# New written orders for the long filter and the mixer's second half, and another place for the throwaway product of the first FFN's modulation sums

## The chip, the cores and the metric

The kernel runs on one core of a Trainium2 chip. The metric is the device time of one execution in microseconds (us). The engines are TensorE (PE, matrix products; PEld is its weight load), VectorE (DVE), ScalarE (ACT) and GpSimd (POOL); SyncE (SP) issues DMAs. The engines run their own instruction lists and wait for each other by semaphores.

## The reference

Two layers of a diffusion transformer over 512 image positions (`x`) and 256 context positions (`ctx`), width 1024. Layer 0 mixes by a Fourier transform and a long convolution, layer 1 by latent attention. Each layer is modulated by vectors that are computed from a condition (`c`, `c_ctx`): six of 1024 each.

```python
def _adaln(cond, w_mod, b_mod):
    mod = jax.nn.silu(cond) @ w_mod + b_mod
    return jnp.split(mod[:, None, :], 6, axis=-1)

def _long_conv(u, spectrum, bias):
    L = u.shape[1]
    y = jnp.fft.irfft(jnp.fft.rfft(u, n=2 * L, axis=1) * spectrum[None], n=2 * L, axis=1)[:, :L]
    return y + u * bias

def _fourier_hyena_mixer(h, w_in, w_out, conv_w, conv_b, w1, b1, w2, b2, w3, b3, w4, freq, hy_bias):
    proj = h @ w_in
    u_f = proj[..., :D_FOURIER].reshape(B, L, 4, 128)
    y_f = jnp.fft.fft2(u_f, axes=(1, 3), norm='ortho').real.reshape(B, L, D_FOURIER)
    u_h = _dwconv3(proj[..., D_FOURIER:], conv_w, conv_b)
    x0, x1, v = jnp.split(u_h, 3, axis=-1)
    spectrum = _hyena_filter_spectrum(L, w1, b1, w2, b2, w3, b3, w4, freq)
    y_h = x0 * _long_conv(v * x1, spectrum, hy_bias)
    return jnp.concatenate([y_f, y_h], axis=-1) @ w_out

def reference(...):
    for i in range(2):
        sh1, sc1, g1, sh2, sc2, g2 = _adaln(c, w_mod[i], b_mod[i])
        hx = _modulate(_rms_norm(x, norm1[i]), sh1, sc1)
        ...
        x = x + g1 * yx
        x = x + g2 * _conv_ffn(_modulate(_rms_norm(x, norm2[i]), sh2, sc2), *ffn)
        ...
    return x
```

The context goes through the same steps with its own modulation (until the last layer's attention).

## The kernel before, in words

**Layout.** Activations lie transposed: 1024 features as eight tiles of 128 partitions, positions along the free axis (512 image columns and 256 of the context, 772 with padding). The tiles `x0` to `x7` of pool `xp` hold the input rows at first. Later in the mixer the first four hold `x0` of the reference, and the last four, called `Uf`, hold the Fourier channels; `Uf[3]` is `x7`.

**Products.** Every large product is made of three: a weight tile is split into a high part `wh` (ACT, L191) and a remainder `wl` (DVE, L196), an activation likewise, and `mm3` issues high by high (L216), high by low (L217) and low by high (L218). A 128 by 1024 weight arrives by an SP DMA as `wr`. Pool `W` keeps three each of `wr`, `wh` and `wl`. Accumulators are `mm` (1024 columns, three buffers) and `ms` (512 columns, two).

**The stages up to the first FFN.** (1) The norm of the input and a small network for the filter, in an order of their own. (2) The *filter*: the filter's taps, their transform, and five of the input projections, which are spread among them. (3) The *remaining in-projections*: seven with a convolution of three taps after each (L432 on ACT, L434 to L436 on DVE), the product and folding of their results, and transposes. (4) The *second half*: projections 11, 6 and 7, the forward transform of the folded product, its multiplication by the spectrum, the inverse transform, and the two transforms of the Fourier channels. (5) The *output projection* `res_proj(0, 2, ...)`: eight rows of `w_out` for the image columns, each closed by a residual addition on DVE (`xr`, L1212) and followed by the next norm's square sums (`nt`, L332), then the context's columns. After that come the first FFN and layer 1.

**What sets the order.** Stages 2 and 4 run in the order of the tables `FILTER_ORDER` and `MIX_ORDER`. Each token is one step, and under `manual_schedule` PE, DVE, ACT and POOL each run their instructions in the order in which the tokens issue them. SP's loads and stages 3 and 5 are placed by the framework. An engine never runs a later instruction of its list past a waiting one.

Tokens of the filter that are spoken of: `MM05` and the like make taps of two tiles; `U0`, `U1` copy Fourier channels out of their accumulators (ACT); `P40` is the first quarter of projection 4; `SPAx2` and `SPBx2` are the two halves of the transform for frequency tile x2, both into one `mm` accumulator; `SDAx2` and `SDBx2` scale these halves into SBUF (DVE, L760); `CB4` and `CC4` are the DVE steps of projection 4's convolution (L790, L792); `G0` to `G5` are modulation blocks.

Tokens of the second half: `P70` to `P73` are quarters of projection 7; `SC0`, `SC1` (context) and `SX0` to `SX3` (image) are tiles of the forward transform, `mm` accumulators all; `DA`, `DB` multiply one by the spectrum (DVE, L985 to L988) and release it; `QA`, `QB` add (POOL); `YA`, `YB` and `LA`, `LB` split the result into high and low (`LA` on DVE, `LB` on POOL); `IC0` to `IC3` and `IX0` to `IX3` are the inverse transform; `FA`, `FB` (image) and `GA`, `GB` (context) are the two transforms of Fourier group 0 to 3, with the splits `PH`/`PL` and `GH`/`GL` between them and the sums `FE`/`FS` and `GE`/`GS` (L1102 to L1109) behind; `TH`, `TL` split the cosine and sine tables `ct`, `st`; `FH`, `FL` split a Fourier group; `ZH`, `ZL` split its result into `yh`, `yl`; `OA` and `OB0` to `OB3` are the output projection's first row. `HP` closes the pools of the projections' inputs, whose space the tables and `y` take.

**Modulation sums.** The modulation of the first FFN and of layer 1 is computed on DVE. `gemv_dve` handles one block of 128 outputs: it multiplies a row block of `wmodT` by the broadcast condition `sb`, sums along the row (L301), for the image's condition and for the context's, and adds the bias (L302). The elementwise product itself isn't needed; it goes to a bf16 tile `junk` of 1024 columns, which has one buffer of its own. 32 blocks belong to layer 0's remaining modulation: sixteen are done up to the start of stage 4, eight more by `hook` after the rows of stage 5, one after each row, and eight in the FFN. `junk` depends on nothing else, so the framework may issue such a sum as soon as its weights can be loaded.

Of the kernel before, what the change touches and what calls it, by code (L numbers as in the profile page):

```python
# [101 lines left out]
Rc0 THc0 THs0 YBx0 YAx0 Rn0 CC7 LBx0 IC2 FL0 TLs0 Rc1 IC3 THn0 LAx0 GA0 DAx1 DBx1 QAx1 SX2 GH0 QBx1 FA0 GL0 TLc0 THc1 YAx1 YBx1
LBx1 LAx1 FH1 TLn0 TLc1 DAx2 DBx2 SX3 PH0 GB0 ICM0 FH2 QAx2 QBx2 PL0 YAx2 ICH0 YBx2 LAx2 FL1 DAx3 GE0 ICE2 LBx2 DBx3 ICL0 FL2 FB0 FA1 FE0 GS0 PH1 QAx3
Ri1 GA1 QBx3 FS0 ICM1 PL1 YBx3 ICH1 FA2 WHi1 ICL1 ICE3 FB1 ICS2 LBx3 WLi1 GH1 YAx3 PH2 GL1 GA2 LAx3 Ro0 FE1 IX1 PL2 GB1 ICS3 ICM2 IXE1 IX0 IXS1 FH3
FS1 ICH2 ICM3 GH2 ICH3 ICL2 IXM1 IXH1 IXE0 ICL3 IX2 GE1 IXS0 FB2 FL3 GS1 IXE2 IXM0 GL2 FA3 FE2 IXH0 IXS2 IX3 IXM2 IXH2 FS2 GA3 PH3 IXL1 IXL0 PL3 IXL2
# [32 lines left out]
class Builder:  # L138
# [152 lines left out]

        return turn

    def gemv_dve(self, i, jt, conds=(0, 1), raw=None):

        nc = self.nc
        raw = raw or self.wraw(self.I["wmodT"][i, jt])
        for j in conds:
# [2 lines left out]
            nc.vector.scalar_tensor_tensor(junk, raw, 1.0, self.sb[:, j, :], op0=ALU.mult, op1=ALU.mult, accum_out=acc)  # L301
            nc.vector.tensor_tensor(self.mod[i][:, jt, j : j + 1], acc, self.col(f"bm_{i}", jt), op=ALU.add)  # L302
# [1899 lines left out]
```

## Time and profile before

| | us |
|---|---|
| runs | 1555.84, 1561.79, 1557.8 |
| median of the runs | 1557.8 |
| the profiled execution, its own time | 1557.68 |
| its span in the profile | 1555.9 |
| filter (stage 2) | 69.1 to 135.6 |
| remaining in-projections (stage 3) | 135.6 to 199.7 |
| second half (stage 4) | 199.7 to 299.5 |
| output projection, image rows (stage 5) | 299.5 to 338 |

The stages are named by PE's first matmul of each. In a row of the timeline stand the start, the duration, the engine, the line, the operation, the tiles written and read, and in brackets how long the engine had been idle before and what ended this. Matmuls are pipelined, so that a row's duration is longer than the distance to the next start. A row of the groups has the count, the busy time, the mean duration in ns, and the idle time before.

### The profile page before, as it was taken

The page shows a single profiled execution, that of the slowest core. Times are in us where ns is not written, and L with a number is a line of the kernel's source. Part 1 is how long each engine was busy: PE and PEld are TensorE (multiplying, and loading weights), DVE is VectorE, ACT ScalarE, POOL GpSimd, SP SyncE. Part 2 cuts the span into 40 slices and gives each one's busy share as a digit, 9 for nine tenths or more (in the row PEclk, how much of TensorE's full clock was granted, in tenths as well). Part 3 has the DMA queues.
Part 4 walks back from the last instruction along what each step waited for, and adds up shares of the span by engine and source line. Part 5 has one row for each costly group of instructions (what it writes and reads, how often), then busy time and mean ns, then how long its engine had stood idle before and what let it go on. Part 6 is the DMA issues. An engine that isn't in the chain of part 4 may idle for free.

```text
span 1555.9 us, 21217 instructions
## 1 busy us (share of the span) xinstructions
PE 1525.5 (98%) x8456; PEld 1271.6 (82%) x8456; DVE 1037.8 (67%) x1755; ACT 604.7 (39%) x875; POOL 95.8 (6%) x110
## 2 busy tenths in 40 slices
PE   7999998999999999999999999999999999999999
PEld 5788888888888888888888897766569888888887
DVE  6699969878988356663365388999977543444343
ACT  4361224424323212322133246989854432233231
POOL 0121135000000000000000000201200000000000
PEclk9999999999999999999999999999999999999999
DMA  9336502542544235441343220000043223322222
GB/s 367 128 108 228 177 26 77 191 134 94 164 163 157 69 108 172 159 142 63 105 156 115 81 78 21 11 14 14 1 136 109 82 97 100 101 95 95 95 83 94
DMA packets 54111, 171.48 MB, mean 110 GB/s; under 512 B 6139, under 2 KB 9533, under 8 KB 52989
## 3 DMA queue, kind: packets, MB, share of 16 engines
q1 hardware_dynamic: 54013, 170.13, 32.9%
q8 instruction: 67, 1.10, 0.3%
q14 instruction: 31, 0.25, 0.1%
HBM read 164.34 MB, written 5.77 MB: 109 GB/s over the span
## 4 chain that ended last, share of the span: by engine, by line
PE 85%; DVE 8%; issue 2%; ACT 2%; DMA 2%; POOL 1%; SPq 0%; ACTq 0%; DVEq 0%; POOLq 0%
PE mm L216 23%; PE mm L217 23%; PE mm L218 23%; PE pv L1733 3%; DVE junk L301 2%; PE s L216 2%; PE pv L1744 1%; PE s L217 1%; PE s L218 1%; DVE wl L196 1%; PE k L216 1%; PE k L217 1%; PE k L218 1%; DMA wr<-wmodT 1%; PE ms L1637 1%
## 5 line engine op out<-in xcount | busy, mean ns | idle before, releaser
L191 ACT ACTIVATE wh<-wr 128x1024 fp32r<-128x1024 f32 (+1 forms) x184 | 189.7, 1034 | 526.8 <-PE mm L217 450.6
L216 PE MATMUL mm<-hh,wh 128*128 128x512 f32 (+1 forms) x856 | 332.5, 388 | 4.2 <-DVE tm L436 1.7
L217 PE MATMUL mm<-hl,wh 128*128 128x512 f32 (+1 forms) x856 | 330.5, 386 | 2.3 <-DVE hl L371 2.3
L218 PE MATMUL mm<-hh,wl 128*128 128x512 f32 (+1 forms) x856 | 330.0, 386 | 0.0
L196 DVE TENSOR_TENSOR wl<-wr,wh 128x1024 fp32r<-128x1024 f32 (+1 forms) x184 | 222.0, 1209 | 127.1 <-ACT wh L191 121.4
L301 DVE SCALAR_TENSOR_TENSOR junk<-wr,sb 128x1024 bf16<-128x1024 f32 x128 | 157.9, 1234 | 54.7 <-DMA wr<-wmodT 54.4
L216 PEld LDWEIGHTS mm<-hh,wh 128*128 128x128 f32 x856 | 160.9, 188 | 37.7 <-issue 5.9
L218 PEld LDWEIGHTS mm<-hh,wl 128*128 128x128 f32 x856 | 160.8, 188 | 32.7
L217 PEld LDWEIGHTS mm<-hl,wh 128*128 128x128 f32 x856 | 160.9, 188 | 32.2 <-DVE hl L371 3.3
L1212 DVE SCALAR_TENSOR_TENSOR xr<-mm,mod,xr 128x512 f32<-128x512 f32 (+1 forms) x88 | 56.0, 652 | 165.5 <-PE mm L218 163.9
L216 PE MATMUL mm<-hhc,wh 128*128 128x256 f32 (+1 forms) x488 | 135.9, 279 | 0.0
L217 PE MATMUL mm<-hlc,wh 128*128 128x256 f32 (+1 forms) x488 | 135.9, 279 | 0.0
L218 PE MATMUL mm<-hhc,wl 128*128 128x256 f32 (+1 forms) x488 | 135.6, 278 | 0.0
L217 PE MATMUL mm<-al,wh 128*128 128x512 f32 x328 | 127.7, 389 | 0.0
L218 PE MATMUL mm<-ah,wl 128*128 128x512 f32 x328 | 127.7, 389 | 0.0
L216 PE MATMUL mm<-ah,wh 128*128 128x512 f32 x328 | 127.6, 389 | 0.0
L216 PEld LDWEIGHTS mm<-hhc,wh 128*128 128x128 f32 x488 | 91.7, 188 | 3.9
L217 PEld LDWEIGHTS mm<-hlc,wh 128*128 128x128 f32 x488 | 91.6, 188 | 3.9
L218 PEld LDWEIGHTS mm<-hhc,wl 128*128 128x128 f32 x488 | 91.9, 188 | 0.0
L1263 DVE TENSOR_TENSOR fg<-fg,mm 128x768 f32<-128x768 f32 (+1 forms) x44 | 36.1, 821 | 74.9 <-PE mm L218 69.3
L1261 ACT ACTIVATE fg<-fg 128x768 f32<-128x768 f32 (+1 forms) x44 | 32.6, 740 | 134.6 <-DVE fg L436 100.5
L218 PEld LDWEIGHTS mm<-ah,wl 128*128 128x128 f32 x328 | 61.6, 188 | 12.8
(441 smaller groups left out, 2808.1 us busy)
## 6 DMA issues: line engine op xcount, KB each, us to landing
wr<-w_up SPq DMA_DIRECT2D x88, 512.0 KB, 3.4
wr<-wmodT SPq DMA_DIRECT2D x80, 512.0 KB, 3.4
wr<-w_dn SPq DMA_DIRECT2D x32, 512.0 KB, 3.4
wm<-wmod0a SPq DMA_DIRECT2D x8, 1024.0 KB, 9.3
wr<-w_in SPq DMA_DIRECT2D x16, 512.0 KB, 3.4
wr<-w_out SPq DMA_DIRECT2D x13, 512.0 KB, 3.6
wr<-w_dn SPq DMA_DIRECT2D x17, 384.0 KB, 3.0
wr<-w_o SPq DMA_DIRECT2D x8, 512.0 KB, 3.5
```

Source lines behind the costliest of these rows:

```text
L191: self.nc.scalar.activation(dst, src, AF.Copy)
L196: (eng or self.nc.vector).tensor_tensor(dst, src, hi.bitcast(F32), op=ALU.subtract)
L216: mmul(out, wh, xh, start=start, stop=False)
L217: mmul(out, wh, xl, start=False, stop=False)
L218: mmul(out, wl, xh, start=False, stop=stop)
L301: nc.vector.scalar_tensor_tensor(junk, raw, 1.0, self.sb[:, j, :], op0=ALU.mult, op1=ALU.mult, accum_out=acc)
L1212: nc.vector.scalar_tensor_tensor(x[m][:, a2:b2], ps[:, a2 + o : b2 + o], mod[:, 8 * sec + m, c : c + 1], x[m][:, a2:b2], op0=ALU.mult, op1 ...
L1261: nc.scalar.activation(g[:, :n], g[:, :n], AF.Silu)
L1263: v.tensor_tensor(a[:, :n], g[:, :n], pss[1][:, :n], op=ALU.mult)
L1637: nc.tensor.matmul(c.s.rt[:, o : o + 2], c.ks[:, t0 : t0 + 128], ksel, start=True, stop=True)
L1733: nc.tensor.matmul(c.P[64 * a : 64 * a + 64, :], V[:, j, o : o + 64], c.S[a, j // 3][:, j % 3, :], start=j == 0, stop=j == 5, tile_positio ...
L1744: nc.tensor.matmul(c.zz[o : o + 32, :], self.ones32, c.S[a, h][:, i, :], start=i == 0, stop=i == 2, tile_position=(0, o))
```

## The change

Three edits. Both tables hold the same tokens as before in another order. `gemv_dve` takes an argument `row`, and with `row="x7"` the throwaway product goes to the first half of a tile in `x7`'s space, so that the sum comes after the last reader of `x7` (`ZH3` and `ZL3`). And `hook` calls it 0, 1, 1, 1, 2, 1, 1, 1 times after rows 0 to 7 instead of once after each. The number of instructions on each engine is the same, and so are their shapes. Line numbers after L90 are lower by two.

```diff
 FILTER_ORDER = """
-R3 WH3 U1 D0 U2 Ra WL3 WHa Rb P30 WLa MM05 P31 D1 R5 PMb0 PMb5 MM42 PMa5 U0 PMa0 P32 P33 HI5 LO5 PMb4 D2 PMb2 SB PMa4
...
-SPBx1 SQc0 WLx2 CSx SPAx1 RCx SSx SPAx2 WLx0 Sx G1 WH4 WL4 SPBx2 SPBx0 P40 NYx P41 SDBx1 SDBx3 SK2 SPAx0 P42 SDAx3 RG2
-SDAx1 G2 SDBx2 RG3 SQx3 G0 G3 KBx3 NDx SQx1 SDAx2 SQx2 WH6 KAx1 WL6 SDAx0 KBx2 KAx2 RG4 G4 P43 KAx3 CA4 SQx0 CB4 CC4
-KBx1 SDBx0
+MM05 Rb U0 U1 SK1 R3 WH3 D2 RG5 WL3 P30 Ra U2 R5 D0 P31 MM42 PMa0 PMb5 WHb P32 SB PMb0 PMa5 D3 G5 HI5 LO5 D1 WHa PMb4 P33 PMa4 RR4 PMa2 RR0 Z4 WLb RG1
...
+NDc SDAc1 SDBc1 WHx3 WLx3 P43 RG4 CA4 SQc1 SPAx3 CSx WLx1 CB5 R6 WHx2 CB4 CC4 WHx0 CC5 RCx WLx2 SPBx3 SSx G0 Sx SPAx1 WLx0 G3 SK2 G4 WH6 SPBx1 SDAx1
+SPAx2 SDBx1 NDx SQx1 SDAx2 SDAx3 SQx2 KAx1 KBx1 SPBx2 WL6 SPAx0 SDBx2 KAx2 SDAx0 SQx0 KBx2 SPBx0 SDBx3 SQx3 SDBx0 KAx3 KBx3
 """
 MIX_ORDER = """
-P11 R6 R7 WH6 WL6 P60 CA11 P61 CB11 CC11 P62 FM Ru0 WH7 FD T3 P63 WHu0 UH CA6 WL7 UL WLu0 CB6 SC0 Ru1 CC6 DBc0 SC1 DAc1 QBc0 YBc0 LBc0 WHu1 Ri0 Rn1
...
+P11 R6 R7 WH6 WL6 Ru0 P60 P61 P62 WHu0 CA11 WLu0 WH7 CB11 CC11 FM FD T3 P63 Rc0 UH UL SC1 WL7 DAc1 QAc1 CA6 P70 P71 DBc1 SC0 FH0 P72 P73 HP THc0 QBc1
+TLc0 CB6 YAc1 LAc1 YBc1 LBc1 FL0 DBc0 DAc0 Rc1 Ri0 THc1 WHi0 QBc0 Rs0 THs0 SX0 CA7 QAc0 YBc0 TLc1 CC6 Ru1 WLi0 TLs0 YAc0 DBx0 LAc0 LBc0 QBx0 DAx0 SX1
+Rn1 YBx0 QAx0 IC1 ICE1 CB7 ICS1 DAx1 GA0 Rn0 IC3 IC0 WHu1 ICM1 THn0 GH0 ICE0 GL0 CC7 ICS0 ICM0 WLu1 THn1 ICE3 LBx0 FA0 QAx1 DBx1 YAx1 FH1 PH0 ICH0
...
+GL3 WHo0 WLo0 GE2 IXH3 IXE0 GB3 IXS0 IXM0 GS2 IXH0 FE3 IXL3 ZH0 IXL0 OA FS3 GE3 ZH1 ZL0 ZH2 OB0 GS3 ZH3 ZL1 ZL2 OB1 OB2 ZL3 OB3
 """
-    def gemv_dve(self, i, jt, conds=(0, 1), raw=None):
+    def gemv_dve(self, i, jt, conds=(0, 1), raw=None, row=None):
...
-            junk = self.t(self.sbp, [P, D], BF16, "junk", 1)
+            junk = self.t(self.xin, [P, TW], F32, row)[:, : D // 2].bitcast(BF16) if row else self.t(self.sbp, [P, D], BF16, "junk", 1)
...
-        xp = self.pool("xp", side="right")
+        xp = self.xin = self.pool("xp", side="right")
...
         def hook(stage, j, m):
             if stage == 0:
-                if len(gl) > 8:
-                    self.gemv_dve(*gl.pop(0))
+                for _ in range((0, 1, 1, 1, 2, 1, 1, 1)[j]):
+                    self.gemv_dve(*gl.pop(0), row="x7")
                 if j == 7:
                     self.make_A(0, 1)
             nhook(stage, j, m)
```

The order on the engines at three places.

PE where the filter's frequency tile x2 goes from its first half (`a0h`, `a0l`) to its second (`a1h`, `a1l`). Before:

```order
L216 MATMUL mm_1156<-a0h_938,wh_1051 128x512
L217 MATMUL mm_1156<-a0l_939,wh_1051 128x512
L218 MATMUL mm_1156<-a0h_938,wl_1052 128x512
L216 MATMUL mm_1156<-a1h_993,wh_1051 128x512
L217 MATMUL mm_1156<-a1l_994,wh_1051 128x512
```

Now:

```order
L214 MATMUL mm_1276<-a0h_968,wh_1189 128x512
L215 MATMUL mm_1276<-a0l_969,wh_1189 128x512
L216 MATMUL mm_1276<-a0h_968,wl_1190 128x512
L214 MATMUL mm_1276<-a1h_1006,wh_1189 128x512 [waits DVE_49]
L215 MATMUL mm_1276<-a1l_1007,wh_1189 128x512
```

The second half's first matmul now waits for DVE, whose reading of the first half (`SDAx2`) is written ahead of it. It is the same at x0.

DVE near the start of the second half, in the forward transform's multiplications (`sx`). Before:

```order
L934 SCALAR_TENSOR_TENSOR x_19_118<-mm_2001,pcol_67,x_19_118 128x771 [waits DVE_49]
L985 TENSOR_TENSOR sx_2096<-mm_2086,s_266_1088 128x512 [waits PE_49]
L986 TENSOR_TENSOR sx_2097<-mm_2086,s_270_1097 128x512
L988 TENSOR_TENSOR sx_2097<-mm_2086,s_262_1055 1x512 [waits DVE_49]
L985 TENSOR_TENSOR sx_2108<-mm_2101,s_256_1042 128x512 [waits PE_49]
L986 TENSOR_TENSOR sx_2109<-mm_2101,s_257_1044 128x512
L196 TENSOR_TENSOR wl_2118<-wr_2093,wh_2117 128x1024 [waits DMAHW2_49,Activation_49]
```

Now:

```order
L984 TENSOR_TENSOR sx_2125<-mm_2085,s_276_1143 128x512
L194 TENSOR_TENSOR ctl_2213<-wr_2081,cth_2212 128x520 [waits DMAHW2_49,PE_49,Activation_49]
L930 SCALAR_TENSOR_TENSOR x_19_118<-mm_2003,pcol_67,x_19_118 128x771
L194 TENSOR_TENSOR s_468_2221<-sx_2093,s_467_2220 128x512 [waits Activation_49]
L194 TENSOR_TENSOR wl_2136<-x_21_120,wh_2135 128x772
L983 TENSOR_TENSOR sx_2229<-mm_2128,s_267_1083 128x512 [waits DVE_49,PE_49]
L984 TENSOR_TENSOR sx_2230<-mm_2128,s_261_1026 128x512 [waits Pool_49]
L986 TENSOR_TENSOR sx_2230<-mm_2128,s_275_1140 1x512 [waits DVE_49]
```

The first split of the cosine table (`ctl`, token `TLc0`) and that of a Fourier group (`wl<-x_21`, `FL0`) now stand between the multiplications of the two context tiles; `ctl` waits for DMA, PE and ACT.

DVE from the end of the second half to the first residual addition (`xr_612`). Before:

```order
L301 SCALAR_TENSOR_TENSOR junk_3164,gacc_3165<-wr_3162,sb_87 128x1024 [waits DMAHW7_49]
L302 TENSOR_TENSOR mod_4_73<-gacc_3165,pcol_67 128x1 [waits DVE_49]
L301 SCALAR_TENSOR_TENSOR junk_3168,gacc_3169<-wr_3162,sb_87 128x1024
L1107 TENSOR_TENSOR x_24_123<-e_2949,mm_2924 128x128 [waits Activation_49]
L1108 TENSOR_TENSOR x_24_123<-e_2949,mm_2924 128x127
L1109 COPY x_24_123<-e_2949 128x1
L196 TENSOR_TENSOR yl_601_2942<-x_21_120,yh_600_2941 128x772 [waits Activation_49]
L196 TENSOR_TENSOR yl_603_2944<-x_22_121,yh_602_2943 128x772 [waits Activation_49]
L196 TENSOR_TENSOR yl_605_2946<-x_23_122,yh_604_2945 128x772 [waits Activation_49]
L196 TENSOR_TENSOR yl_607_2948<-x_24_123,yh_606_2947 128x772 [waits Activation_49]
```

Now:

```order
L194 TENSOR_TENSOR yl_599_2934<-x_21_120,yh_598_2933 128x772 [waits PE_49,Activation_49]
L1105 TENSOR_TENSOR x_24_123<-e_2970,mm_2916 128x128 [waits Activation_49]
L1106 TENSOR_TENSOR x_24_123<-e_2970,mm_2916 128x127
L1107 COPY x_24_123<-e_2970 128x1
L194 TENSOR_TENSOR yl_601_2936<-x_22_121,yh_600_2935 128x772 [waits Activation_49]
L194 TENSOR_TENSOR yl_603_2938<-x_23_122,yh_602_2937 128x772 [waits Activation_49]
L194 TENSOR_TENSOR yl_605_2940<-x_24_123,yh_604_2939 128x772 [waits Activation_49]
L299 SCALAR_TENSOR_TENSOR x_658_3110,gacc_3111<-wr_3108,sb_87 128x1024 [waits DMAHW4_49,DVE_49]
L1210 SCALAR_TENSOR_TENSOR xr_612_3018<-mm_2954,mod_4_73,xr_612_3018 128x512 [waits DMAHW0_49,PE_49]
```

The modulation sums write to `x_658` (the space of `x7`) instead of `junk`, and all stand behind the last split of `yl`. Before, six of them (three blocks) stood among the second half's steps.

More of the change, by code (lines that the diff above doesn't have):

```diff
@@ L90 @@
 FILTER_ORDER = """
-R3 WH3 U1 D0 U2 Ra WL3 WHa Rb P30 WLa MM05 P31 D1 R5 PMb0 PMb5 MM42 PMa5 U0 PMa0 P32 P33 HI5 LO5 PMb4 D2 PMb2 SB PMa4
-AB5 MM31 SK1 RR4 RR0 PMa2 WHb Z4 D3 HI4 MX5 U3 LO4 RG1 SPAc0 WLb AB4 SPBc0 RG5 Z0 PMb1 Rx3 MX4 HI2 WH5 Rx1 PMa1 PMb3
-SPAc1 Rx2 SPBc1 PMa3 HI1 HI3 LO2 Rx0 WL5 Qc CSc NYc LO1 RCc AB2 P50 P51 HI0 SSc AB1 G5 WHx3 Sc LO3 MX2 P52 R4 R6 LO0
-WLx3 AB0 SDAc1 SDBc1 WHx1 AB3 WHx2 SQc1 NDc P53 CA5 MX3 SPAx3 MX0 SDBc0 WLx1 MX1 Q23 WHx0 SDAc0 SPBx3 CB5 CC5 Q01 Qx RG0
-SPBx1 SQc0 WLx2 CSx SPAx1 RCx SSx SPAx2 WLx0 Sx G1 WH4 WL4 SPBx2 SPBx0 P40 NYx P41 SDBx1 SDBx3 SK2 SPAx0 P42 SDAx3 RG2
@@ L96 @@
-SDAx1 G2 SDBx2 RG3 SQx3 G0 G3 KBx3 NDx SQx1 SDAx2 SQx2 WH6 KAx1 WL6 SDAx0 KBx2 KAx2 RG4 G4 P43 KAx3 CA4 SQx0 CB4 CC4
-KBx1 SDBx0
+MM05 Rb U0 U1 SK1 R3 WH3 D2 RG5 WL3 P30 Ra U2 R5 D0 P31 MM42 PMa0 PMb5 WHb P32 SB PMb0 PMa5 D3 G5 HI5 LO5 D1 WHa PMb4 P33 PMa4 RR4 PMa2 RR0 Z4 WLb RG1
+AB5 PMb2 R4 Rx1 RG2 HI4 WLa Rx3 MM31 LO4 MX5 U3 PMa3 PMa1 SPAc1 AB4 NYc MX4 HI2 PMb3 WH5 SPBc1 SPBc0 PMb1 Rx0 Z0 G1 Qc CSc HI1 Rx2 WH4 HI3 WL5 RCc
+SPAc0 LO1 LO3 LO2 RG0 P50 HI0 AB3 LO0 WL4 AB1 SSc Sc RG3 SDAc0 G2 AB0 P51 P52 NYx P53 SDBc0 WHx1 AB2 MX2 MX1 MX3 Q23 P40 MX0 P41 P42 SQc0 Q01 Qx CA5
@@ L98 @@
+NDc SDAc1 SDBc1 WHx3 WLx3 P43 RG4 CA4 SQc1 SPAx3 CSx WLx1 CB5 R6 WHx2 CB4 CC4 WHx0 CC5 RCx WLx2 SPBx3 SSx G0 Sx SPAx1 WLx0 G3 SK2 G4 WH6 SPBx1 SDAx1
+SPAx2 SDBx1 NDx SQx1 SDAx2 SDAx3 SQx2 KAx1 KBx1 SPBx2 WL6 SPAx0 SDBx2 KAx2 SDAx0 SQx0 KBx2 SPBx0 SDBx3 SQx3 SDBx0 KAx3 KBx3
 """
 MIX_ORDER = """
-P11 R6 R7 WH6 WL6 P60 CA11 P61 CB11 CC11 P62 FM Ru0 WH7 FD T3 P63 WHu0 UH CA6 WL7 UL WLu0 CB6 SC0 Ru1 CC6 DBc0 SC1 DAc1 QBc0 YBc0 LBc0 WHu1 Ri0 Rn1
-P70 QAc1 YAc1 WLu1 P71 DAc0 P72 QAc0 P73 YAc0 WHi0 SX0 LAc1 DBc1 HP QBc1 Rs0 LAc0 WLi0 SX1 CA7 YBc1 THn1 LBc1 CB7 DBx0 IC0 QBx0 ICE0 DAx0 ICS0 IC1 QAx0 ICE1 TLn1 ICS1 FH0
@@ L102 @@
[L102 to L105, printed above, removed]
@@ L106 @@
-IXE3 IXS3 GB2 WHo0 IXM3 IXH3 FB3 GH3 GE2 FE3 WLo0 GL3 GB3 GE3 ZH0 IXL3 GS2 FS3 GS3 OA ZL0 OB0 ZH1 ZL1 ZH2 ZH3 OB1 ZL2 ZL3 OB2 OB3
+P11 R6 R7 WH6 WL6 Ru0 P60 P61 P62 WHu0 CA11 WLu0 WH7 CB11 CC11 FM FD T3 P63 Rc0 UH UL SC1 WL7 DAc1 QAc1 CA6 P70 P71 DBc1 SC0 FH0 P72 P73 HP THc0 QBc1
+TLc0 CB6 YAc1 LAc1 YBc1 LBc1 FL0 DBc0 DAc0 Rc1 Ri0 THc1 WHi0 QBc0 Rs0 THs0 SX0 CA7 QAc0 YBc0 TLc1 CC6 Ru1 WLi0 TLs0 YAc0 DBx0 LAc0 LBc0 QBx0 DAx0 SX1
+Rn1 YBx0 QAx0 IC1 ICE1 CB7 ICS1 DAx1 GA0 Rn0 IC3 IC0 WHu1 ICM1 THn0 GH0 ICE0 GL0 CC7 ICS0 ICM0 WLu1 THn1 ICE3 LBx0 FA0 QAx1 DBx1 YAx1 FH1 PH0 ICH0
@@ new lines @@
+QBx1 IC2 LAx1 PL0 TLn0 SX2 YAx0 ICL0 ICE2 TLn1 ICS3 ICM3 GB0 GE0 GS0 ICH3 YBx1 LBx1 Ri1 ICH1 FB0 FL1 FA1 FE0 DBx2 QBx2 PH1 FS0 YBx2 DAx2 LAx0 SX3 FH2
+PL1 GA1 GH1 LBx2 FB1 QAx2 WHi1 DAx3 Ro0 ICS2 FE1 QAx3 YAx2 GL1 DBx3 GB1 FL2 GA2 YAx3 FS1 QBx3 FA2 YBx3 PH2 ICL1 WLi1 LAx2 ICM2 ICH2 LAx3 PL2 LBx3 IX1
+IX2 IXE1 GH2 IXS1 GE1 GL2 IXE2 FB2 ICL2 GS1 FH3 FE2 IX3 IXM1 IXH1 ICL3 IXS2 FL3 IXM2 GA3 FA3 IXE3 IXL1 FS2 IXH2 IXS3 GB2 IXM3 IXL2 PH3 IX0 PL3 FB3 GH3
+GL3 WHo0 WLo0 GE2 IXH3 IXE0 GB3 IXS0 IXM0 GS2 IXH0 FE3 IXL3 ZH0 IXL0 OA FS3 GE3 ZH1 ZL0 ZH2 OB0 GS3 ZH3 ZL1 ZL2 OB1 OB2 ZL3 OB3
```

## The prediction, made before the changed kernel ran

> **What bounds the kernel now.** I read the page first: busy shares, then the chain of waits.
>
> ```profile
> span 1555.9 us, 21217 instructions
> PE 1525.5 (98%) x8456; PEld 1271.6 (82%) x8456; DVE 1037.8 (67%) x1755; ACT 604.7 (39%) x875; POOL 95.8 (6%) x110
> PE 85%; DVE 8%; issue 2%; ACT 2%; DMA 2%; POOL 1%; SPq 0%; ACTq 0%; DVEq 0%; POOLq 0%
> ```
>
> PE sets the end, and the change takes no matmul away. So only PE's waits and its clock can move the time. By the order, the rows that move on PE and DVE lie between some 60 and 340 us; the rest of the program reads alike. I cut that stretch into its stages (filter, remaining in-projections, second half, output projection), and a part of the second half into pieces. A row has the window and its length, then the busy time (and instructions) of PE, PEld, DVE, ACT and POOL, the granted clock, the DMA share and GB/s.
>
> ```profile
> 69.10:135.60 66.50, 66.50 (x335) 52.27 (x334) 57.49 (x94) 30.17 (x46) 14.27 (x10) 1.00 0.42 139
> 135.60:199.70 64.10, 60.88 (x355) 53.55 (x354) 57.69 (x103) 15.49 (x17) 9.62 (x7) 1.00 0.58 193
> 199.70:299.50 99.80, 92.93 (x599) 84.08 (x598) 87.46 (x150) 42.59 (x71) 30.87 (x36) 0.97 0.23 75
> 299.00:338.00 39.00, 39.00 (x170) 31.62 (x170) 27.26 (x51) 9.51 (x12) 0.00 (x0) 1.00 0.62 207
> 236.56:239.97 3.41, 2.38 (x22) 2.27 (x21) 3.41 (x9) 2.34 (x6) 2.94 (x2) 1.00 0.00 0
> 239.97:243.38 3.41, 3.41 (x18) 3.41 (x17) 3.41 (x6) 1.36 (x3) 3.41 (x2) 0.50 0.42 123
> 243.38:246.80 3.42, 3.42 (x12) 2.84 (x11) 3.23 (x6) 2.24 (x4) 2.60 (x3) 0.50 0.10 38
> ```
>
> The filter has no PE idle to give: 66.50 of 66.50. The in-projections lack some 3.2 us, the second half some 6.9, and the output projection nothing. In the second half PE also ran 6.83 us at a granted clock of 0.50, behind a piece in which it was busy 2.38 of 3.41 us; full speed would save at most half, 3.4 us. The single waits, with what ended them:
>
> ```profile
> 144.25 0.47 PE L216 MATMUL mm<-hh,wh 128*128 128x512 f32 x1 [0.30 <-DVE x L792]
> 171.84 0.47 PE L216 MATMUL mm<-hh,wh 128*128 128x512 f32 x1 [1.68 <-DVE tm L436]
> 190.69 0.47 PE L216 MATMUL mm<-hh,wh 128*128 128x512 f32 x1 [1.24 <-ACT tm L432]
> 218.27 0.50 PE L218 MATMUL mm<-uTh,wl 128*128 128x512 f32 x1 [0.46 <-DVE wl L196]
> 238.69 0.30 PE L216 MATMUL ms<-wh,s 128*128 128x128 f32 x1 [1.03 <-DVE e L1029]
> 260.58 0.36 PE L216 MATMUL mm<-csh,wh 128*128 128x256 f32 x1 [1.21 <-DVE x L1108]
> 263.79 0.39 PE L216 MATMUL mm<-cth,pqh 128*128 128x258 f32 x1 [0.83 <-DVE pql L196]
> 290.81 0.37 PE L216 MATMUL mm<-cth,pqh 128*128 128x130 f32 x1 [1.49 <-DVE pql L1081]
> 296.39 0.50 PE L217 MATMUL mm<-yl,wh 128*128 128x512 f32 x1 [0.96 <-DVE yl L196]
> ```
>
> All but one are ended by DVE. The largest gain to be had is then 3.22 us of waits in the in-projections and 5.98 + 3.4 = 9.4 in the second half, 12.6 in all.
>
> **The change part by part.** *Filter, end.* In the new table DVE's scaling SDAx2 of one half of a frequency tile is written before PE's SPBx2, and SDAx0 before SPBx0, and the order shows the first matmul of each second half with a wait on DVE. Before, both halves ran through. A round trip is built from these rows:
>
> ```profile
> 101.19 0.40 PE L217 MATMUL mm<-a0l,wh 128*128 128x512 f32 x1
> 101.43 0.39 PE L218 MATMUL mm<-a0h,wl 128*128 128x512 f32 x1
> L760 DVE TENSOR_TENSOR s<-mm,S 128x512 f32<-128x512 f32 x11 | 7.2, 682 | 0.0
> 143.09 1.02 DVE L792 SCALAR_TENSOR_TENSOR x<-mm,pcol,x 128x771 f32<-128x771 f32 x1
> ```
>
> Matmuls start 0.24 us apart but last 0.40, so draining costs 0.16; the convolution that ends at 144.11 releases PE at 144.25, a handover of 0.14, paid twice; the scaling takes 0.68. That is 1.1 each, 2.2 for both, if DVE stands ready. It may not: the stage has it busy 57.49 of 66.50 us, and one modulation sum of 1.22 (row below) in front of either scaling would add that. Bounds +2.2 and +5; I take +2.6, near the free round trip, since the order has a wait on PE at the scaling and no sum between it and the PE work it follows for x2. *Filter, start:* taps before the fourth projection, with two copies first that ACT (30.17 of 66.50 busy) hides: 0, and by the nearest row of a stage that waited for its first operand, 0.46, if they are late.
>
> *In-projections.* The convolution steps CB4, CC4 and the sum G4 go ahead of the filter's last scalings, so DVE enters this stage with less behind it. The waits of 0.30 and 1.68 are for convolutions that DVE finishes late: I take −2.0 (bounds −2.0 and 0). The 1.24 is for ACT, whose order stays.
>
> *Second half, what goes.* Six sums, three blocks of modulation, leave its queue; they go to rows of the output projection. Their first and last start here, with the rows they collide with:
>
> ```profile
> 266.72 1.22 DVE L301 SCALAR_TENSOR_TENSOR junk<-wr,sb 128x1024 bf16<-128x1024 f32 x1
> 293.78 1.22 DVE L301 SCALAR_TENSOR_TENSOR junk<-wr,sb 128x1024 bf16<-128x1024 f32 x1
> L302 DVE TENSOR_TENSOR mod<-gacc,pcol 128x1 f32<-128x1 f32 x6 | 0.9, 158 | 0.1
> L196 DVE TENSOR_TENSOR ctl<-wr,cth 128x520 fp32r<-128x520 f32 x2 | 1.9, 940 | 0.0
> L196 DVE TENSOR_TENSOR s<-sx,s 128x512 fp32r<-128x512 f32 x6 | 4.7, 778 | 0.7 <-ACT s L191 0.7
> L985 DVE TENSOR_TENSOR sx<-mm,s 128x512 f32<-128x512 f32 x12 | 8.1, 678 | 0.0
> L932 DVE SCALAR_TENSOR_TENSOR x<-mm,pcol,x 128x771 f32<-128x771 f32 x2 | 2.0, 1014 | 0.2 <-ACT x L930 0.2
> L196 DVE TENSOR_TENSOR wl<-x,wh 128x772 fp32r<-128x772 f32 x4 | 4.9, 1224 | 0.0
> 246.91 1.57 POOL L196 TENSOR_TENSOR s<-sx,s 128x512 fp32r<-128x512 f32 x1 [0.74 <-ACT s L191]
> 247.25 1.79 DVE L196 TENSOR_TENSOR stl<-wr,sth 128x520 fp32r<-128x520 f32 x1
> 238.47 0.67 DVE L196 TENSOR_TENSOR stl<-wr,sth 128x504 fp32r<-128x504 f32 x1
> ```
>
> That is 6 × 1.22 + 0.9 = 8.2 us of a DVE that has 87.46 of 99.80 filled. It would pay for the waits at 260 to 296 (4.5 us together), which the table also attacks by issuing the splits of the cosine and sine tables (TLc0, TLs0, TLc1) and FL0 earlier. So the most that can come back is the 9.4.
>
> *Second half, what comes.* The earlier splits stand in front of work that PE awaits. TLc0's row waits on PE, for the projection P71 whose inputs' space it writes; DBc0 and DAc0, which free the accumulator of SX0, stand behind it. From P71's end DVE has ctl 0.94, CB6 1.01, LAc1 0.78, FL0 1.22 and five products of 0.68: 7.35 us. PE has SC0, six steps of 0.24, and two quarters of a projection, an estimated 2.1 each (a quarter has six steps of 0.24 and six of half the columns): 5.6. SX0 then waits up to 1.8; I take 1.5, since neighbours on DVE overlap by 0.08 each. By the same count IC1 waits for LAc0 behind TLc1, CC6, WLi0 and TLs0 between 0 and 1.3 (0.6), FA0 for GL0 and SX2 for WLu1 0.4 each, and GB0 for TLn0 0.5 to 2.3 (1.4). What I see no reason to lose are the old 0.46 at the transform's start and the 0.96 at the end: together 5.7, so this stage gives 9.4 − 5.7 = 3.7. Bounds: −9.4 if every wait goes, +0.7 if the early splits meet POOL's multiplications. For that two rows speak: a split took 1.79 us while POOL subtracted, and 0.67 elsewhere (520 and 504 columns); 1.1 more on each of the four is 4.4, and 5.7 + 4.4 − 9.4 = 0.7.
>
> The Trainium skill, "SBUF — State Buffer", section "Who interferes with whom", says that a DVE operation with two SBUF inputs excludes a GpSimd one that reads SBUF, whichever is first. It speaks against this change, which puts four such splits where POOL has work; the 1.79 beside 0.67 agrees with it, and by it this stage ends at its upper bound.
>
> *Output projection.* Eight blocks instead of five, sixteen sums. Its rows:
>
> ```profile
> L301 DVE SCALAR_TENSOR_TENSOR junk<-wr,sb 128x1024 bf16<-128x1024 f32 x10 | 12.2, 1223 | 0.5 <-DMA wr<-wmodT 0.5
> L196 DVE TENSOR_TENSOR wl<-wr,wh 128x1024 fp32r<-128x1024 f32 x6 | 7.4, 1226 | 0.7 <-ACT wh L191 0.6
> L1212 DVE SCALAR_TENSOR_TENSOR xr<-mm,mod,xr 128x512 f32<-128x512 f32 x8 | 6.0, 752 | 9.3 <-PE mm L218 7.9 <-DMA xr<-xT 1.4
> L332 DVE TENSOR_TENSOR nt<-nt,nt 128x512 f32<-128x512 f32 x7 | 4.8, 691 | 2.0 <-ACT nt L325 2.0
> 332.55 0.75 DVE L1212 SCALAR_TENSOR_TENSOR xr<-mm,mod,xr 128x512 f32<-128x512 f32 x1 [1.69 <-PE mm L218]
> 338.11 0.75 DVE L1212 SCALAR_TENSOR_TENSOR xr<-mm,mod,xr 128x512 f32<-128x512 f32 x1 [3.35 <-PE mm L218]
> ```
>
> PE's row takes 338.11 − 332.55 = 5.56 us. DVE's takes two sums with their adds (2.76), a split (1.23), a residual (0.75) and a square sum (0.69), 5.43. The row with two blocks is 2.6 over, and the weights, split about a row ahead, cover that; DVE was busy only 27.26 of 39.00, and three blocks add 8.3. Cost 0, at most +4 if the cover is gone: the next split would come late by the 2.6, and a sum's DMA adds to it. The sums' DMAs stand in SP's queue among the weight loads as before. That their product goes to x7's space rather than the throwaway tile costs nothing by itself; it only keeps them behind the mixer's last readers of x7.
>
> Sum: +2.6 − 2.0 − 3.7 + 0 = −3.1. The profiled execution took 1557.68 us (its span is 1555.9), and the median of the runs shown is 1557.8, so nothing needs shifting: **1554.6 us**.
>
> **The rivals.** *The clock halves again,* +3.4: 1558.0. For it: the transforms of 128 columns that preceded the low clock remain, and SX0 and IC1 wait near them. Against: the table spreads them among other products. The Trainium skill, "TensorE: Matmul & The Clock Gate", section "Part 1: The HAM clock gate", halves the clock after an idle window of 3413 ns. The 6.83 us agree with two such windows; but the piece before was busy 2.38 of its 3.41 us, so an idle one was not needed. By the rule this rival would not come at all.
>
> *DVE is freed altogether,* so that no new wait lasts: 1557.68 − 9.4 − 2.0 + 2.2 = 1548.5. For it: 8.2 us leave the queue. Against: each early split is in front of something.
>
> *Slower: the output projection becomes DVE's.* It decides where a DVE row exceeds 5.56 us, 0.13 above my count. If each block waits 1.5 us for its weights from memory, the row is 6.9, and eight rows cost 8 × 1.4 = 11, against the gains of 3.1: 1565.6. For it: one such DMA wait of 0.5 is there already. Against: DVE's idle time, 11.7 us of the 39.00.
>
> *The early work blocks more than I took:* filter +5, second half +0.7 with its splits held up by POOL, in-projections −2.0: 1561.4. For it: DVE's 57.49 of 66.50 in the filter. Against: both stages would have to end at their upper bounds. That the change doesn't do what it says, sums still entering the second half, is excluded by their place in the order behind x7's last reader.
>
> **How the numbers follow.** Forecast 0.45, low clock 0.17, DVE freed 0.17, output projection 0.07, early work blocking 0.14. Half a per cent, 7.8 us, is about what a measurement here can tell from no change. Faster than that is most of the second rival, 0.15; slower is half of the output projection's case, 0.04, and the blocking with a low clock on top, 0.05: 0.09; the rest, 0.76, is the same. The range reaches from 1548.3 to 1562.5, and leaves out nearly half of the freed case, the output projection's and the worst of the blocking: the likeliest case's own range is 1551 to 1558.
>
> **What would show it.** Matmul waits on DVE of about a microsecond at the head of SPBx2 and SPBx0, near 128 and 133 us (else the first term is wrong); no wait above 1 us on a convolution of DVE in the in-projections; no modulation sum before the last split of yl; a granted clock of 1.00 through the second half; a wait for SX0 near 230 us and for GB0 later; the stage in 96 us rather than 99.8; output rows still 5.56 apart. I am wrong if DVE is idle in the second half while PE waits, or if rows of the output projection stretch.

## The result, and the profile after

The changed kernel takes 1570.25 us (median of 5 runs, 1568.62 to 1571.49), the kernel before in the same session 1557.93 (5 runs, 1555.84 to 1561.79): 1.0071 times the time, 95% interval 1.0059 to 1.0083. That is 12.3 us slower, where 3.1 us faster was forecast.

The page of the changed kernel, the rows that answer to those of before:

```profile
span 1568.5 us, 21204 instructions
PE 1531.0 (98%) x8456; PEld 1276.9 (81%) x8456; DVE 1034.8 (66%) x1755; ACT 604.8 (39%) x875; POOL 94.6 (6%) x110
PE 92%; DVE 3%; DMA 2%; ACT 1%; issue 1%; SPq 1%; POOL 0%; DVEq 0%; ACTq 0%; POOLq 0%
```

The span grew by 12.6 us (1568.5 against 1555.9) and PE's busy time by 5.5, so PE both waited more and ran slower in places. For each kernel the table lays the first matmul of each stage in the profiled execution beside the same one of before (69.14 us to the filter, 130.57 for filter and in-projections, 99.80 for the second half up to the last step OB3, 438.07 from there to a fixed matmul in the first FFN, 248.47 to one in layer 1's attention, 569.85 for the rest) and shows each stage's difference in us:

| kernel | to the filter | filter and in-projections | second half | output projection, FFN | layer 1, first part | rest |
|---|---|---|---|---|---|---|
| changed | +11.80 | +0.78 | −4.26 | +1.43 | +3.56 | −0.75 |
| sk1_early | +10.19 | +0.13 | −0.03 | −0.30 | 0.00 | −0.01 |
| sk1_back | +2.65 | +1.09 | −5.92 | +0.33 | +3.71 | +0.02 |
| no_trip | +0.20 | −1.16 | −4.27 | +1.44 | +3.73 | −0.79 |
| ring_k | −0.13 | −0.07 | −5.86 | −0.04 | +1.37 | −0.78 |
| sums_only | +1.21 | +0.45 | −2.19 | +1.81 | −0.03 | −0.02 |
| tables_only | +0.53 | +0.48 | −2.34 | +1.43 | +3.66 | −0.77 |
| hyb_early | +1.84 | +0.13 | −4.65 | +0.02 | +3.37 | −0.01 |
| warm20 | +8.55 | +1.11 | −4.49 | +1.59 | +6.88 | −0.06 |
| tlc0_late | +1.05 | −0.87 | −5.12 | +0.01 | +1.42 | −0.05 |
| b_k | +1.34 | −0.21 | 0.00 | −0.14 | +3.63 | −0.75 |
| mix_ring | +0.33 | −0.34 | −4.20 | +1.33 | +0.35 | −0.71 |

The mark between the third column and the fourth is OB3's last matmul. In PE's list three matmuls of the next row stand ahead of it in the kernel before, one in the kernels with the new table of the second half, and none in sums_only. At 0.23 us each, 0.46 us (sums_only: 0.69) went from one column to the next without being gained or lost: for equal work the changed kernel's two entries are −3.8 and +1.0.

Read the first row: the stages on which the prediction spent its sum came out near its numbers (+0.78 and −4.26). The loss lies ahead of them and behind them, in the norm and the start of the projections (before 81 us) and in layer 1 (near 958 us).

**Ahead of the filter.** DVE's timeline of the changed kernel, then PE's:

```profile
36.09 0.48 DVE L369 SCALAR_TENSOR_TENSOR hlc<-s,mod,hhc 128x256 fp32r<-128x256 f32 x1
44.92 1.07 DVE L738 TENSOR_SCALAR brow<-brow 128x512 f32<-128x512 f32 x1 [8.35 <-DMA brow<-hyb]
45.91 1.21 DVE L194 TENSOR_TENSOR wl<-wr,wh 128x1024 fp32r<-128x1024 f32 x1
47.04 0.74 DVE L369 SCALAR_TENSOR_TENSOR hl<-s,mod,hh 128x512 fp32r<-128x512 f32 x1
```

```profile
38.21 0.39 PE L214 MATMUL mm<-hh,wh 128*128 128x512 f32 x1
47.84 0.79 PE L215 MATMUL mm<-hl,wh 128*128 128x512 f32 x1 [9.23 <-DVE hl L369]
48.43 0.63 PE L216 MATMUL mm<-hh,wl 128*128 128x512 f32 x1
```

L738 is the token SK1: DVE scales `brow`, the bias row `hyb` that a DMA spreads over the partitions. In the old table it stood behind MM31; in the new one it is the fifth token, and the first that has work for DVE. The framework put it into DVE's list between two of the input norm's steps. There it waited 8.35 us for its DMA, and behind it stood the remainder `hl` that PE needed. SP's queue shows where the row's load stood:

```profile
29.76 0.85 SPq L265 DMA_DIRECT2D wm<-wmod0a  x2
32.09 0.42 SPq L619 DMA_DIRECT2D brow<-hyb  x1
```

It was issued at 32.09 us behind the large `wm` loads, and DVE went on at 44.92. (In hyb_early, where it is issued ahead of them, it landed 6.2 us after its issue.) Then the clock. These windows of the changed kernel are read as those of the prediction: length, busy time of PE, PEld, DVE, ACT and POOL, the granted clock.

```profile
39.11:42.52 3.41, 0.00 (x0) 0.00 (x0) 0.00 (x0) 0.00 (x0) 0.00 (x0) 1.00 1.03 396
42.52:52.76 10.24, 4.92 (x15) 4.16 (x16) 7.84 (x13) 2.18 (x4) 2.52 (x2) 0.50 0.57 216
```

With nothing to do from 38.6 us on, PE was granted half its clock from 42.52 to 52.76. 4.92 us of matmuls ran in it, which at full speed would be about half as long: an estimated 2.5 us more. Of the wait, 0.59 us was there before. 9.23 − 0.59 + 2.5 = 11.1 of the 11.8.

**In layer 1.** PE's and DVE's timelines of the changed kernel:

```profile
958.38 0.45 PE L214 MATMUL k<-wh,qah 128*128 128x384 f32 x1 [2.38 <-DVE kp L1527]
```

```profile
957.32 1.00 DVE L1527 SCALAR_TENSOR_TENSOR kp<-mm,pcol,ropeK 64x768 f32<-64x768 f32 x1
```

and the same two of the kernel before:

```profile
946.01 0.42 PE L216 MATMUL k<-wh,qah 128*128 128x384 f32 x1
```

```profile
947.58 1.00 DVE L1529 SCALAR_TENSOR_TENSOR kp<-mm,pcol,ropeK 64x768 f32<-64x768 f32 x1
```

The code is the same, and so is the place in both lists. Before, the product ran 1.6 us ahead of `kp`; now it waits for it. PE's list says that it waits for another engine:

```
before  L216 MATMUL k_1577_8878<-wh_8799,qah_8478 128x384 [waits Activation_49]
changed L214 MATMUL k_1577_8878<-wh_8799,qah_8478 128x384 [waits DVE_49]
```

`kp` reads the last accumulator `mm` of the pool that layer 1 closes just ahead, and `k` belongs to the pool that takes its banks. In the compiled programs this `mm` and `k` lie in banks 0 and 4 before, and both in bank 4 in the changed kernel.

A low clock of 3.41 us followed, at 964 us, but not from this wait. In the window just ahead of it PE was busy throughout, mostly with products of 32 and 64 partitions:

```profile
960.71:964.12 3.41, 3.41 (x20) 2.58 (x20) 2.36 (x4) 1.66 (x3) 0.00 (x0) 1.00 0.02 5
960.69 1.49 PE L1534 MATMUL ms<-ones,sqpe 32*128 32x1 f32 x12
962.11 1.55 PE L1536 MATMUL s<-kp,msk 64*128 64x512 f32 x4
```

The kernel before has the same products without a low clock (the last section comes back to this). So the wait is 2.38 of the 3.56 us.

**In the stages between.** PE's waits of the changed kernel, up to 375 us, in total us, times and longest:

```profile
PE mm L214 <- DVE s L758: 2.2, 1, 2.2
PE mm L214 <- DVE sx L984: 2.1, 1, 2.1
```

The first is SPBx2 at 141.02 us, the second SX0 at 243.12. Behind each came one window of half clock, a third at 302 us in the output projection's first row, and a fourth at 370 us, where its last columns meet the first FFN. For the second half the sums are: PE's waits of over 0.1 us were 6.8 us before and 3.5 in the changed kernel, and 6.83 us ran at half clock in both.

### The profile page after: what moved, and what is told of

Its sections match the earlier page's. It is cut to its first block, busy times and chain, and to the rows that moved or that the text cites. A ratio compares the mean times of both kernels' runs of the same rounds, so it can differ in the third digit from the quotient of the medians.

```text
span 1568.5 us, 21204 instructions
## 1 busy us (share of the span) xinstructions
PE 1531.0 (98%) x8456; PEld 1276.9 (81%) x8456; DVE 1034.8 (66%) x1755; ACT 604.8 (39%) x875; POOL 94.6 (6%) x110
## 4 chain that ended last, share of the span: by engine, by line
PE 92%; DVE 3%; DMA 2%; ACT 1%; issue 1%; SPq 1%; POOL 0%; DVEq 0%; ACTq 0%; POOLq 0%
PE mm L214 26%; PE mm L215 25%; PE mm L216 25%; PE pv L1731 3%; PE s L214 2%; PE pv L1742 1%; PE s L216 1%; PE s L215 1%; DMA wr<-w_in 1%; PE k L214 1%; DMA brow<-hyb 1%; PE k L215 1%; PE k L216 1%; PE ms L1635 1%; DVE wl L194 1%
## 5 line engine op out<-in xcount | busy, mean ns | idle before, releaser
L299 DVE SCALAR_TENSOR_TENSOR junk<-wr,sb 128x1024 bf16<-128x1024 f32 x112 | 137.1, 1224 | 58.0 <-DMA wr<-wmodT 57.8
```

## The experiments

Times are medians beside the kernel before on the same chip. A kernel's own runs spread by up to 9 us, and the half-clock windows of 3.41 us fall in other places from one execution to the next, so differences below about 1.5 us are not read from medians.

**sk1_back: the changed kernel with SK1 at its old place**

```diff
-MM05 Rb U0 U1 SK1 R3 WH3 ... MM31 LO4 ...
+MM05 Rb U0 U1 R3 WH3 ... MM31 SK1 LO4 ...
```

> The changed kernel with one token, SK1 (DVE's scaling of the broadcast bias row brow), put back behind MM31 in the new filter table. Theory 1: written early, SK1 became the first DVE step of its table, the framework put it into DVE's list ahead of the input norm's steps, and DVE stood 8.35 us waiting for brow's DMA, PE 9.23 us behind it, and then PE ran at half clock for 10.24 us. Then this run has no PE wait above 1 us before 60 us, the clock stays 1.00 there, the filter starts at 70 us rather than 80.9, and the time falls from 1570.25 by about 11: 1559 (1557.5 to 1560.5). Rival: the early loss is that of transfers landing later (the first w_in landed some 0.8 us later and the filter's tables are loaded in another order), whatever SK1 does: then the filter still starts behind 76 us and the time stays above 1566.

1559.59 us, 1.0008 times before (0.9999 to 1.0017). One token gives back 10.7 us (10.2 if each kernel is taken against the kernel before on its own chip); PE's waits on `hl` are 2.3 us again, as in the kernel before:

```profile
PE mm L216 <- DVE hl L370: 2.3, 3, 0.9
PE ms L337 <- DVE s L331: 2.2, 1, 2.2
```

The filter began at 71.80 us instead of 69.14. 0.9 of this came in the norm of the input rows, where the second row belongs and where such differences came and went between kernels that are alike. The rest came with a window of half clock at 27 us. SK1 has no part in either.

**sk1_early: the kernel before with SK1 moved up**

```diff
-R3 WH3 U1 D0 U2 ... AB5 MM31 SK1 RR4 ...
+R3 WH3 U1 SK1 D0 U2 ... AB5 MM31 RR4 ...
```

> The kernel before with SK1 alone moved, to behind U1 near the start of the old filter table. Theory 1 expects most of the loss here too: a PE wait of 8 to 10 us before 50 us, some 10 us of half clock, and 1558 + 11 = 1569 (1566 to 1571). The rival (transfers) expects no change: 1557 to 1559.

1567.93 us, 1.0061 (1.0045 to 1.0078). The one token costs the kernel before 10.4 us, all of it ahead of the filter (+10.19), with the same window of half clock of 10.24 us. Taking the token out and putting it in agree.

**hyb_early: the changed kernel, brow's DMA issued right behind the input rows**

```diff
+            nc.sync.dma_start(self.brow, I["hyb"].partition_broadcast(P))
             wm = [self.gemv_raw(0), self.gemv_raw(1)]
...
-            nc.sync.dma_start(self.brow, I["hyb"].partition_broadcast(P))
```

> The changed kernel, with SK1 as early as the change put it, but brow's DMA issued 16 transfers sooner, right behind the loads of the input rows. Theory: what costs is the wait for the transfer, not the place of the instruction or its 0.4 to 1 us; with the row there in time PE's wait of 9.23 us and the low clock near 50 us are gone, and the time is that of sk1_back, 1559.6 (1558.5 to 1562; the other loads are pushed back by the 256 KB of this one). Rival: an early SK1 holds DVE up wherever it stands: above 1565.

1561.7 us, 1.0022 (1.0010 to 1.0034). SK1 went even further up DVE's list, into the norm, and waited there too, but shortly:

```profile
18.43 0.43 DVE L738 TENSOR_SCALAR brow<-brow 128x512 f32<-128x512 f32 x1 [1.23 <-DMA brow<-hyb]
```

Some 8.5 to 9.5 us came back with the instruction as early as ever. The wait for the transfer costs, not the place by itself. The framework seems to place the instruction where it reckons with the row's arrival; that was not tested.

**warm and warm20: throwaway matmuls in the gap**

```diff
             both(2, 0)
+            spare(20)
             first(0, 1)
```

> The changed kernel with 80 more throwaway matmuls of 128x256 (0.11 us each) on PE ahead of the product that waited 9.23 us, into an accumulator that is overwritten later. Theory: the wait for brow stays, but PE is busy in it, so the clock isn't halved; the 4.9 us of PE work that ran at half clock between 47.8 and 52.8 us come back by half: the filter starts about 2.4 us earlier and the time is 1567.8 (1567 to 1569). Rival: the clock falls for another reason, or the matmuls hold PE up: 1570 or more.

1595.47 us, 1.0232 (1.0216 to 1.0247): the matmuls took 0.43 us each, two records for one, so 80 were 34 us of work. They were far longer than the gap, so that the time says nothing on the theory; the clock did stay at 1.00 from 20 to 324 us. With 20:

> As the run warm, with the size mended: one of these throwaway matmuls took 0.43 us there, not 0.11, so 80 of them were 34 us of work in a gap of 9; now 20, 8.6 us. Theory: the wait for brow stays, PE is busy in it, the clock stays 1.00, and the work behind it comes 2.4 us earlier: 1567.8 (1566.8 to 1569). Rival: the clock falls anyway, 1570 or more.

1570.24 us, 1.0066 (1.0053 to 1.0080). The profiled execution shows the theory's part, and why its time did not follow:

```profile
38.08:46.52 8.44, 8.44 (x42) 7.43 (x41) 2.07 (x3) 0.00 (x0) 2.53 (x2) 1.00 1.01 366
956.37:966.61 10.24, 10.24 (x32) 8.09 (x31) 3.31 (x5) 2.64 (x5) 1.69 (x3) 0.50 0.00 0
```

With PE busy in the gap the clock stayed at 1.00 until 297 us, and the filter began at 77.69 us, 3.25 earlier than in the changed kernel. In that execution layer 1 ran three windows at half clock instead of one and took 3.3 us more. The median of the four runs did not fall, so the clock's share of 2.5 us is shown in the stage and not in the total.

**no_trip: sk1_back without the scalings between the halves**

```diff
-... SPAx2 SDBx1 NDx SQx1 SDAx2 SDAx3 SQx2 KAx1 KBx1 SPBx2 WL6 SPAx0 SDBx2 KAx2 SDAx0 SQx0 KBx2 SPBx0 ...
+... SPAx2 SPBx2 SDBx1 NDx SQx1 SDAx2 SDAx3 SQx2 KAx1 KBx1 WL6 SPAx0 SPBx0 SDBx2 KAx2 SDAx0 SQx0 KBx2 ...
```

> As sk1_back (SK1 put back behind MM31), and in the filter table SPBx2 and SPBx0 written right behind SPAx2 and SPAx0 and so ahead of the scalings SDAx2 and SDAx0; PE's and DVE's own lists keep their order there, only the wait of the second half on the first half's scaling goes. Theory: the one PE wait of some 2.1 us for the scaling at SPBx2 is gone, and with it the half-clock window of 3.4 us that followed it: 1559.6 - 2.1 to 3.8 = 1556.5 (1555.5 to 1557.8). Rival: PE waits for something else at the end of the filter (the last weight split, the first remaining projection), and the time stays 1559 to 1560.

1557.21 us, 0.9996 (0.9985 to 1.0007): 2.4 less than sk1_back, which ran on another chip. No wait is left at SPBx2. Part came back as a wait in the in-projections, which sk1_back has at 0.20 and 0.40 us:

```profile
170.76 0.47 PE L215 MATMUL mm<-hh,wh 128*128 128x512 f32 x1 [1.10 <-ACT wh L190]
189.73 0.47 PE L215 MATMUL mm<-hh,wh 128*128 128x512 f32 x1 [1.36 <-DVE tm L435]
```

ring_k, with the same two tables, has them at 2.01 and 1.59 us. DVE's steps stand there in the order of the changed kernel, so those waits had not gone because DVE was ahead, as the prediction said: where PE waits at SPBx2 they are short, where it doesn't they are back. The first of them is now for ACT.

**ring_k and b_k: other banks for layer 1's first accumulator**

```diff
+            K2 = self.ring(psB, [P, 1024], "k2", 1)
             S1 = self.ring(psB, [P, 512], "s", 3)
             MS = self.ring(psB, [P, 512], "ms", 1)
-            K2 = self.ring(psB, [P, 1024], "k2", 1)
             PV = self.ring(psB, [P, 512], "pv", 2)
```

On top of no_trip this takes the wait away:

> As no_trip, and in layer 1 the accumulator k2 is created ahead of the rings s and ms, so that its banks are not those that the rope part's accumulator holds. Theory: in the changed kernel the first product into k waits 2.4 us for DVE's rope product (kp) only because other table orders made the framework give that accumulator other banks; the low clock near 950 us follows from it. Then layer 1 loses the 3.5 us again: no_trip - 3.5 = 1553 (1552 to 1554.5), about 4.5 us faster than the kernel before. Rival: that wait is set by DVE's own lateness in layer 1, and the time equals that of no_trip.

1555.77 us, 0.9977 (0.9966 to 0.9989). The wait of 2.38 us was gone, and layer 1's first part was 1.37 over before instead of 3.73, which is that wait; a window of half clock was still there, at 945 us. So that low clock doesn't need the wait, against the expectation, and the total fell by 1.4 and not by 3.5.

In the kernel before, the same edit moves `k` onto the bank that `kp` reads (both in bank 0; in ring_k they lie in 0 and 4):

> The kernel before with nothing changed but the order in which layer 1 creates its accumulators: k2 ahead of the rings s and ms, so that k2 now gets the banks that hold the rope part's accumulator. Theory: this alone makes the first product into k wait 2.4 us for DVE's kp, and a window of low clock follows in part of the executions: 1557.9 + 2.4 to 3.7 = 1561 (1560 to 1562). Rival: PE's wait there is hidden by other work, and the time stays 1557 to 1559.

1562.26 us, 1.0026 (1.0017 to 1.0034). The wait appears:

```profile
949.62 0.44 PE L216 MATMUL k<-wh,qah 128*128 128x384 f32 x1 [2.38 <-DVE kp L1529]
```

Layer 1's first part took 3.63 us more, as in the changed kernel (3.56), again with one window of half clock. The bank that `mm` has at the end follows from the order in which the tables take and free accumulators: sums_only, with the old tables, doesn't have this wait, and every kernel here with both new ones has it unless the pool's order is changed.

**sums_only and tables_only: the third edit apart from the tables**

sums_only has both old tables; tables_only has both new ones (SK1 at its old place) with the old hook and `junk`.

> The kernel before with the third edit alone: both old tables, the modulation sums in x7's space and the new counts after each row. Theory from the prediction: 8.2 us leave a DVE that had no break from 245 to 299 us, so the waits of 1.21, 0.83 and 1.49 us at 260, 263 and 291 us shrink, the second half ends 3 to 4 us earlier, the output projection holds its 5.56 us a row, and the time is 1554.5 (1553 to 1556.5). Rival 1: the output projection's rows stretch by sums that wait for their weights: 1558 to 1566. Rival 2: those waits are set by the order of the table and not by the sums: 1557 to 1559.

1557.69 us, 0.9995 (0.9986 to 1.0005). The second half was 2.19 us shorter, 1.5 for equal work, and the output projection lost as much: two of its rows took 6.03 and 6.64 us instead of 5.56. The stretch in sums_only, then a row of DVE and one of PE:

```profile
299.00:338.00 39.00, 37.95 (x163) 30.23 (x162) 33.69 (x68) 9.41 (x12) 0.00 (x0) 1.00 0.71 232
311.39 1.23 DVE L301 SCALAR_TENSOR_TENSOR x<-wr,sb 128x1024 bf16<-128x1024 f32 x1 [3.93 <-DMA wr<-wmodT]
328.88 0.50 PE L218 MATMUL mm<-yh,wl 128*128 128x512 f32 x1 [0.83 <-DVE wl L196]
```

DVE's 33.69 us would fit into 39.00; one sum that waited 3.93 us for its weights made the splits behind it late. This is the slower rival, at a seventh of its price.

> As sk1_back without the third edit: both new tables (SK1 put back), the modulation sums in junk and once after each row, so that again four or six of them stand among the steps of the second half. In sk1_back the second half was 5.9 us shorter than before, in sums_only 2.2. Theory: the table does 3 to 4 of it by itself and the sums the rest, which the output projection gives back in part: 1559.6 to 1561.5, the second half 3 to 4.5 us shorter than before. Rival: without room on DVE the new table is worth nothing, and the early splits cost: second half as before, 1563 or more.

1561.37 us, 1.0021 (1.0009 to 1.0033). For equal work the tables shorten the second half by 1.9, the sums by 1.5, both together by 3.8 (changed, no_trip, mix_ring) to 5.5 (sk1_back, ring_k). PE's waits there add up to 6.8 us in tables_only, as in the kernel before, to 4.9 in sums_only and 3.5 with both; what the tables gained alone is one window of half clock less, and the 5.5 is the 3.8 with one window less. In the new tables the third edit is worth 1.8 us (sk1_back against tables_only, on two chips), near the limit of what the medians tell.

**tlc0_late: the early splits behind DBc0 and DAc0 (on ring_k)**

```diff
-TLc0 CB6 YAc1 LAc1 YBc1 LBc1 FL0 DBc0 DAc0 Rc1 ...
+CB6 YAc1 LAc1 YBc1 LBc1 DBc0 DAc0 TLc0 FL0 Rc1 ...
```

> As ring_k, and in the second half's table the splits TLc0 and FL0 are written behind DBc0 and DAc0 instead of ahead of them. In every kernel with the new table PE waited 2.06 us for DVE's last product of DAc0 at SX0, and a 3.4 us window of half clock followed. Theory from the prediction: this wait is the price of the splits in front, 0.94 + 1.22 us; then it falls below 0.3 us, and the time by 2 to 3.5: 1555.8 - 2.7 = 1553 (1552 to 1554.5). Rival: what is late is then the table itself or IC1 some us later, and the time stays 1555 to 1557.

1556.52 us, 0.9992 (0.9979 to 1.0005): no gain over ring_k. The 2.06 us at SX0 were gone, and what comes next was late in their place:

```profile
232.11 0.47 PE L216 MATMUL mm<-uTh,wh 128*128 128x512 f32 x1 [0.70 <-DVE x L934]
237.10 0.33 PE L218 MATMUL ms<-wh,s 128*128 128x128 f32 x1 [1.82 <-DVE s L196]
```

SX1 waits 0.70 for a convolution and IC1 1.82 for LAc0, 2.5 together.

**mix_ring: the old filter table with the new table of the second half**

The third edit stays, and layer 1 creates its accumulators in the order pv, s, ms, k2, with which `k` doesn't wait for `kp`.

> The old filter table with the new table of the second half, the third edit, and layer 1's accumulators created in an order (pv, s, ms, k2) that doesn't make k wait for kp. It takes the new filter table away from the best version so far (ring_k, 1555.8). Theory: the new filter table without SK1's and the scalings' waits is worth nothing, since the filter and the remaining in-projections together took 130.5 us in ring_k and 130.6 before: 1555.8 (1554 to 1557). Rival: the in-projections' shorter waits are worth 2 us: 1558.

1554.44 us, 0.9971 (0.9962 to 0.9980), the lowest median of all, though its interval overlaps ring_k's: 0.3% below the kernel before. The new filter table, without its two faults, shows no gain.

## Why the prediction was wrong, point by point

- *What bounds the kernel.* Right that only PE's waits and clock count. The step that failed is the sentence that the rows which move lie between some 60 and 340 us, and that the rest reads alike. DVE's list in the changed kernel has SK1 among the norm's steps, near 37 us, with a wait on a DMA; PE's list has another engine's wait in layer 1. Both stood in the order, and neither entered the sum.
- *Filter, start.* Forecast 0 to +0.46; the stretch ahead of the filter grew by 11.8. Of all tokens moved up, the term counted PE's taps and ACT's copies and left SK1 out. It should have asked what SK1 reads, when that lands, and what is queued behind it on DVE. sk1_early and sk1_back give 10.4 and 10.2 to 10.7 us for it.
- *Filter, end.* Forecast +2.6 for two round trips. One came, of 2.23 us at SPBx2, and a window of half clock after it; at SPBx0 PE waited for nothing. *In-projections:* forecast −2.0. The waits of 1.68 and 1.24 were absent in the changed kernel and a 0.39 came. Together +0.6 was forecast and +0.78 measured, but no_trip shows the reason wrong: without the round trip the waits return (1.10 and 1.36). That the two terms met the measured sum was luck.
- *Second half.* Forecast −3.7, measured −4.26 (−3.8 for equal work), by luck of its parts. The 3.4 us of the low clock that the sum took as gained did not come: two windows again. Of the 5.7 us of losses 3.5 came. The largest new wait was the one named, SX0, 2.06 where 1.5 was taken, and tlc0_late shows that the splits in front cause it; IC1, FA0, SX2 and GB0 did not wait. And the prediction's list of waits left out one of 0.84 us at 257.69 us, so that 6.8 and not 6.0 could go.
- *Early splits against POOL.* The split TLc0, which stood ahead of the steps that free SX0's accumulator, took 1.83 us where the sum took 0.94, with POOL multiplying at its side:

```profile
235.22 1.83 DVE L194 TENSOR_TENSOR ctl<-wr,cth 128x520 fp32r<-128x520 f32 x1 [1.40 <-ACT s L189]
235.21 1.29 POOL L991 TENSOR_TENSOR sx<-sx,sx 128x512 f32<-128x512 f32 x1
```

  This may be what made SX0's wait longer than forecast (not tested). The stage still ended far inside its upper bound of +0.7.
- *Output projection.* Forecast 0, and with the new tables its rows stayed 5.55 us apart; the 0.46 us up to the last of its image rows are the matmuls that stand on the other side of the mark. With the old tables it lost 1.6 (sums_only), within the bound of +4.
- *Layer 1.* No term; +3.56. A table that frees accumulators in another order moved the banks of a later pool, and PE waited 2.38 for it; b_k and ring_k show this alone. The rest came with a window of half clock.
- *The rival of the low clock* held in kind: the second half again has two windows, and the filter one. *The slower rival* that decided was not among those named.

## What to carry to other kernels

When a written order is changed, follow every token that moved up to what it reads from memory and to what stands behind it on its engine: a 0.4 us instruction whose result is first read some 70 us later cost over 10, because it waited for a transfer and everything behind it in DVE's list waited with it. Compare the lists with their waits over the whole program and not only where the rows move, since allocation order can change which banks, and so which engine, a far later instruction waits for. A wait removed from a stage with other late work behind it moves on (no_trip, tlc0_late), so price the next one as well.
